# Second attention of a two-network kernel: queries and keys projected with the tokens moving and rotated across partitions, all values projected first

## Chip, cores and metric

One NeuronCore of a Trainium2 chip. The metric is the device time of one execution in microseconds, the median of several runs. The program is one launch: it reads float32 inputs and weights from HBM and writes one output of 256 tokens by 1024.

## The reference

A first block (three mixers, gates, a gated feed-forward layer) and then a second network of two layers, each a mixer and a squared-ReLU MLP, with a norm ahead of and behind each part. Mixer 0 is a retention, mixer 1 the attention that is changed here. With 256 tokens and blocks of 256 it has one block, so its selected part adds only terms that are masked:

```python
q, k, v = jnp.split(h @ w_in, 3, axis=-1)          # 8 heads of 128 each
q = partial_rope(q, pos) * (Dh ** -0.5)
k = partial_rope(k, pos)
...
def partial_rope(x, pos):                          # half = 16, ROPE_DIM = 32
    ...
    x1 = x[..., :half].astype(jnp.float32)
    x2 = x[..., half:ROPE_DIM].astype(jnp.float32)
    rot = jnp.concatenate([x1 * cos - x2 * sin, x2 * cos + x1 * sin], axis=-1)
    return jnp.concatenate([rot.astype(x.dtype), x[..., ROPE_DIM:]], axis=-1)
...
s_own = jnp.einsum('bhnid,bhnjd->bhnij', qb, kb).astype(jnp.float32)
s_own = jnp.where(causal, s_own, NEG)
...                                                # softmax, then p_own @ v
return o.astype(h.dtype) @ w_out
```

So of each head's 128 dimensions the first 16 and the next 16 are rotated against each other by an angle that depends on the token; the other 96 stay.

## The kernel before

**Arithmetic.** Every large product keeps float32 precision by splitting both operands in a high and a low part (float32r): hi·hi + hi·lo + lo·hi. Weights come from HBM in units of 512 KB into six raw buffers. ScalarE writes the high part (whi, a copy), VectorE the low part (wlo = raw - whi), into eight buffers each. `weight(key)` splits three units ahead (AHEAD) of the one it returns; a unit's buffers come free when its last matmul is done (`release`).

**Two ways to project 256 tokens on a chunk of 512 columns.** Two tiles t of 128 are held transposed in hT, high and low part side by side.

- `rows_proj` holds a tile's tokens as stationary operand and moves 512 weight columns: three matmuls of 512 for each of 8 k and each t (`mm3`), 48 for a chunk. The result has tokens in partitions.
- `cols_proj` holds 128 weight columns and moves the tokens: one matmul of 512 columns (both parts of hT) with whi and one of 256 with wlo, for each k, 64 for a chunk. The result has output dimensions in partitions; `two_blocks` does it for two blocks of 128 and adds the two halves (ScalarE copies one, VectorE adds).

**The stage.** Six chunks: values, queries and keys for two groups of four heads, ("m", "v"/"q"/"k", 0 or 1). `keep_split_tile` projects a value tile with rows_proj and writes its split form. `part_rope` (L1406) does a query or key tile: rows_proj into a PSUM tile pj; ScalarE copies the 96 plain dimensions times the token's norm factor; VectorE makes two products with frope (cosine and sine times the factor) into rp and two sums; `heads_T` transposes the four heads on TensorE into a PSUM tile mx, and ScalarE copies them to qT or kT, for queries with the scale 128^-0.5. `probs` then makes logits (two heads at a time, TensorE), adds the causal mask on VectorE, does the softmax, transposes the probabilities and splits them; `mix` multiplies with the values and splits the result into ym. The output projection wo1 (`out_proj`) takes head k of ym with unit k.

The order in the program: v0 and q0 for tile 0, then `flush()` (the MLP's Post chain of tile 1: norm, residual, transposes into hT), then v0 and q0 for tile 1; k0; probs and mix of group 0; q1; k1; probs of group 1; v1; mix of group 1; wo1; Post; the MLP's up chunks 0 and 1 with rows_proj. The factor of a tile (`factors[t]`) is computed by `post.rows(t)`, behind the transposes.

**Who sets the order.** The kernel is recorded twice. The first recording goes to a planner (`Plan`), which knows a cost for each instruction and the dependences, and issues, on each engine, the instruction with the lowest program number among those that are ready (Post chains are advanced by 4000, `urgent`). The order so found is then issued as it stands: each engine runs its own list in order. All instructions are recorded through one line, L213, so the profile's groups are told apart by tiles and shapes. Tiles: pj and mx are PSUM (four buffers each), t is the shared scratch t2 (six buffers), y is hT, ym and split values, p is p4 (qT, kT, probabilities and others), fac the norm factors, sm small statistics, const the constants; "mx<-const,t" is a transpose by the identity.

Of the kernel before, what the change touches and what calls it, by code (L numbers as in the profile page):

```python
# [27 lines left out]
AF = mybir.ActivationFunctionType  # L28
# [273 lines left out]
def host_consts():  # L302
    f = np.float32
    p = np.arange(128)
    s, t = p[:, None], p[None, :]
    same = (s // 64) == (t // 64)
    parts = {}
    parts["ident"] = (s == t).astype(f)
    parts["tri64"] = (same & (s <= t)).astype(f) / f(16)
    parts["late64"] = (same & (s > t)).astype(f) / f(16)  # L310
    parts["ind64"] = (p[:, None] // 64 == np.arange(2)[None, :]).astype(f) / f(16)
    parts["tri"] = (s <= t).astype(f)
    parts["ones"] = np.ones((128, 128), f)
    parts["cmask"] = np.concatenate([np.zeros((128, 128), f), np.where(t > s, f(NEG), f(0))], 1).astype(f)
    pos = np.arange(256, dtype=f)
    inv = np.power(f(500000.0), -np.arange(0, 32, 2, dtype=f) / f(32)).astype(f)
    ang = (pos[:, None] * inv[None, :]).astype(f).astype(np.float64)
    cs = np.stack([np.cos(ang), np.sin(ang)], 1).astype(f)
    parts["rope"] = cs.reshape(2, 128, 2, 16).transpose(1, 0, 2, 3).reshape(128, -1)
    lg = np.log(f(1.0) - np.exp2(-5.0 - np.arange(4, dtype=f)).astype(f)).astype(f)  # L320
    dec = np.zeros((128, 4, 2, 128), f)
    for h in range(4):
        g = np.float64(lg[h])
        dec[:, h, 0] = np.where(t >= s, np.exp(g * np.maximum(t - s, 0)), 0.0)
        dec[:, h, 1] = np.exp(g * (t + 1.0)) * np.exp(g * (127.0 - s))
    parts["dec"] = (dec / 16.0).reshape(128, -1).astype(f)
    freq = (f(1.0) / np.power(f(10000.0), np.linspace(0.0, 1.0, 128, dtype=f))).astype(f)
    ang = (freq[:, None] * pos[None, :]).astype(f).astype(np.float64)
    parts["rot"] = np.concatenate([np.cos(ang), np.sin(ang)], 1).astype(f)
    at, n = {}, 0  # L330
    for k, v in parts.items():
        at[k] = (n, v.shape[1])
        n += v.shape[1]
    return np.ascontiguousarray(np.concatenate(list(parts.values()), 1)), at
# [32 lines left out]
def network(ctx, tc, I, consts, c_at, out, after=None):  # L367
# [30 lines left out]
    def f32(ap):  # L398
        return ap.bitcast(F32)
# [72 lines left out]
    add_chunk("wo0", I["w_out_0_2"], 0, 1024, per=1, nk=16)  # L472
    add_mlp(0)
    base1 = dict(q=0, k=1024, v=2048)
    for kind, j in (("v", 0), ("q", 0), ("k", 0), ("q", 1), ("k", 1), ("v", 1)):
        add_chunk(("m", kind, j), I["w_in_1_2"], base1[kind] + 512 * j, 512)
    add_chunk("wo1", I["w_out_1_2"], 0, 1024, per=1)
    add_mlp(1)

# [15 lines left out]
    def pump(upto):  # L495
        while state["split"] <= min(upto, len(units) - 1) and state["split"] < state["done"] + NSPL:
            i = state["split"]
            load_to(i + NRAW - 1)
            src, kt, n, deint, gain = units[i]
            raw = raws.pop(i)  # L500
            hi = sbt([128, UNIT], "whi", NSPL, F32R)[:, :kt * n]
            lo = sbt([128, UNIT], "wlo", NSPL, F32R)[:, :kt * n]
            if deint:
                src4 = raw.rearrange("p (k m c) -> p k c m", k=kt, c=2)
                hi4, lo4 = [a.rearrange("p (k c m) -> p k c m", k=kt, c=2) for a in (hi, lo)]
                for k in range(kt):
                    S.activation(hi4[:, k], src4[:, k], AF.Copy)
                    V.tensor_tensor(lo4[:, k], src4[:, k], f32(hi4[:, k]), op=OP.subtract)
            elif gain is not None:
                for k in range(kt):  # L510
                    split(hi[:, k * n:(k + 1) * n], lo[:, k * n:(k + 1) * n], raw[:, k * n:(k + 1) * n],
                          g_col[:, gain + k:gain + k + 1])
            else:
                split(hi, lo, raw)
            spl[i] = (cols(hi, n), cols(lo, n))
            state["split"] += 1
        load_to(state["split"] + NRAW - 1)
# [225 lines left out]
    def probs(qT, kT, kind, hp, bias=None):  # L743
# [4 lines left out]
        for t in range(2):  # L748
# [4 lines left out]
            if kind == "cross":  # L753
                L = sp
            else:
                L = cols(t2(), 256)
                if kind == "fox":
                    V.tensor_tensor(L[:, :, :W], sp[:, :, :W], bias[t][:, 2 * hp:2 * hp + 2, :W], op=OP.subtract)
                else:
                    V.tensor_tensor(L[:, :, :W], sp[:, :, :W],  # L760
                                    cmask[:, None, 256 - W:].to_broadcast([128, 2, W]), op=OP.add)
            m, nm, l, r = small(2), small(2), small(2), small(2)
            V.tensor_reduce(m, L[:, :, :W], axis=AX, op=OP.max)
            V.tensor_scalar(nm, m, -1.0, None, op0=OP.mult)
# [636 lines left out]


    plan.table(nc, "natural_log_exp_and_others")
    rope = const("rope").rearrange("p (t c n) -> p t c n", t=2, c=2)
    frope = sbt([128, 2, 2, 16], "frope", 1)
    def part_rope(key, t, dst, scale):  # L1406
        p = pj()
        rows_proj(key, hT, t, p, 0, 512)
        src = cols(p, 128)
        q = t2()  # L1410
        qh = cols(q, 128)
        S.activation(qh[:, :, 32:], src[:, :, 32:], AF.Copy, scale=factors[t][0])
        a, b = [sbt([128, 4, 2, 16], "rp", 4) for _ in range(2)]
        for o, c in ((a, 0), (b, 1)):
            V.tensor_tensor(o, src[:, :, :32].rearrange("p h (c n) -> p h c n", c=2),
                            frope[:, t, c][:, None, None, :].to_broadcast([128, 4, 2, 16]), op=OP.mult)
        V.tensor_tensor(qh[:, :, :16], a[:, :, 0], b[:, :, 1], op=OP.subtract)
        V.tensor_tensor(qh[:, :, 16:32], a[:, :, 1], b[:, :, 0], op=OP.add)
        heads_T(q, dst, t, scale)

    QS = float(128 ** -0.5)
    ym = []
    v, qT, kT = new_v(), cols(p4(), 256), cols(p4(), 256)
    for t in range(2):
        if t:
            flush()
        V.tensor_scalar(frope[:, t], rope[:, t], factors[t][0], None, op0=OP.mult)
        keep_split_tile(v, ("m", "v", 0), hT, t, factors[t][0])
        part_rope(("m", "q", 0), t, qT, QS)
    release_chunk(("m", "v", 0), 4)  # L1430
    release_chunk(("m", "q", 0), 4)
    for t in range(2):
        part_rope(("m", "k", 0), t, kT, None)
    release_chunk(("m", "k", 0), 4)
    ym.append(new_y())
    for hp in range(2):
        mix(probs(qT, kT, "moba", hp), v, ym[0], "moba", hp)
    qT, kT = cols(p4(), 256), cols(p4(), 256)
    for kind, dst, sc in (("q", qT, QS), ("k", kT, None)):
        for t in range(2):  # L1440
            part_rope(("m", kind, 1), t, dst, sc)
        release_chunk(("m", kind, 1), 4)
    pTs = [probs(qT, kT, "moba", hp) for hp in range(2)]
    v = keep_split(("m", "v", 1), hT, [f for f, _ in factors])
    ym.append(new_y())
    for hp in range(2):
        mix(pTs[hp], v, ym[1], "moba", hp)
# [72 lines left out]
```

## Time and profile before

| | us |
|---|---|
| median of 3 runs | 1137.17 (1136.91 to 1137.51) |
| the profiled execution | 1138.05 |
| its span in the trace | 1136.3 |
| TensorE busy | 1125.8 |
| VectorE busy | 822.5 |
| ScalarE busy | 649.9 |
| GpSimd busy | 6.0 |

Busy times are unions of the listed durations. Matmuls overlap their neighbours, so a matmul's cost is read as the distance from its start to the next one's. The stage lies between about 838 and 947 us of the span. Times in the rows count from the start of the span.

### The profile page before, as it was taken

The numbers are of one execution on the slowest core, as the hardware profiler recorded it, in microseconds if no ns is written. First come the engines' busy times: TensorE is split into PE (matmuls) and PEld (weight loads), VectorE is DVE, ScalarE is ACT, GpSimd is POOL, SyncE is SP. The second block draws the span as 40 slices with busy tenths as digits, with TensorE's granted clock in tenths as the row PEclk, the third lists the DMA queues.
The fourth block names the chain that finished last, engine by engine and source line by source line (L and its number), as shares of the span: only waits on it lengthen the run. The fifth ranks groups of instructions, "written<-read, shape, count | busy, mean of one in ns | idle before, by whom it ended". The sixth has DMA issues, their size and how long they took to land.

```text
span 1136.3 us, 15881 instructions
## 1 busy us (share of the span) xinstructions
PE 1125.8 (99%) x5852; PEld 953.1 (84%) x5852; DVE 822.5 (72%) x1487; ACT 649.9 (57%) x1068; POOL 6.0 (1%) x18
## 2 busy tenths in 40 slices
PE   9999999999999999999999999999999999999997
PEld 7989888888988888888888888888888888888885
DVE  6998797897656566787858497656588889755564
ACT  6867657675645554646556474545466667545451
POOL 1000000000000000000000000000000000000000
PEclk9999999999999999999999999999999999999999
DMA  8654546665666664665464448564637354665631
GB/s 306 212 161 125 164 136 184 217 227 172 204 187 191 190 192 127 198 211 186 150 209 159 134 161 281 167 206 152 217 118 254 115 175 136 223 192 185 215 113 38
DMA packets 100756, 204.23 MB, mean 180 GB/s; under 512 B 6533, under 2 KB 30150, under 8 KB 100678
## 3 DMA queue, kind: packets, MB, share of 16 engines
q1 hardware_dynamic: 99814, 202.17, 55.1%
q10 hardware_dynamic: 864, 1.05, 0.3%
q8 instruction: 46, 0.75, 0.3%
q14 instruction: 32, 0.26, 0.1%
HBM read 202.14 MB, written 1.05 MB: 179 GB/s over the span
## 4 chain that ended last, share of the span: by engine, by line
PE 94%; DVE 2%; DMA 2%; ACT 1%; issue 0%; SPq 0%; DVEq 0%; ACTq 0%
PE pj L213 62%; PE mx L213 32%; DVE wlo L213 1%; DMA p<-in_ln_mlp_post_dram 1%; DMA raw<-in_w_in_dram 1%; DMA raw<-in_w_down_dram 1%; DVE p L213 0%; DVE t L213 0%; ACT whi L213 0%; DVE sm L213 0%; SPq L213 0%; ACT t L213 0%; DMA x<-in_x_dram 0%; DVE y L213 0%; DVE x L213 0%
## 5 line engine op out<-in xcount | busy, mean ns | idle before, releaser
L213 PE MATMUL pj<-whi,y 128*128 128x512 f32 (+2 forms) x1744 | 543.6, 388 | 0.0
L213 DVE TENSOR_TENSOR wlo<-raw,whi 128x1024 fp32r<-128x1024 f32 (+1 forms) x326 | 378.0, 1170 | 125.6 <-ACT whi L213 121.4
L213 ACT ACTIVATE whi<-raw 128x1024 fp32r<-128x1024 f32 (+1 forms) x326 | 327.1, 1019 | 122.3 <-PE pj L213 91.2
L213 PEld LDWEIGHTS pj<-whi,y 128*128 128x128 f32 x1744 | 321.7, 188 | 65.9 <-issue 0.3
L213 PE MATMUL pj<-wlo,y 128*128 128x512 f32 (+2 forms) x872 | 337.3, 387 | 0.6 <-DVE wlo L213 0.6
L213 PE MATMUL mx<-y,whi 128*128 128x512 f32 x672 | 236.8, 396 | 0.0
L213 PEld LDWEIGHTS pj<-wlo,y 128*128 128x128 f32 x872 | 164.0, 188 | 33.2 <-DVE wlo L213 1.4
L213 PE MATMUL mx<-y,wlo 128*128 128x256 f32 x672 | 188.5, 281 | 0.0
L213 PEld LDWEIGHTS mx<-y,whi 128*128 128x128 f32 x672 | 126.1, 188 | 29.9
L213 PE MATMUL pj<-y,whi 128*128 128x512 f32 x416 | 146.3, 395 | 0.0
L213 PEld LDWEIGHTS mx<-y,wlo 128*128 128x128 f32 x672 | 126.5, 188 | 0.8
L213 PE MATMUL pj<-y,wlo 128*128 128x256 f32 x416 | 116.5, 280 | 0.0
L213 PEld LDWEIGHTS pj<-y,whi 128*128 128x128 f32 x416 | 78.1, 188 | 18.1
L213 DVE SCALAR_TENSOR_TENSOR wlo<-raw,gcol,whi 128x512 fp32r<-128x512 f32 (+2 forms) x120 | 85.0, 747 | 5.5 <-ACT whi L213 3.8
L213 ACT ACTIVATE t<-mx 128x256 f32<-128x256 f32 (+1 forms) x106 | 41.5, 396 | 81.4 <-PE mx L213 81.2
L213 ACT ACTIVATE whi<-raw,gcol 128x512 fp32r<-128x512 f32 (+2 forms) x120 | 79.8, 719 | 14.4 <-PE pj L213 10.7
L213 PEld LDWEIGHTS pj<-y,wlo 128*128 128x128 f32 x416 | 78.2, 188 | 0.1
L213 DVE TENSOR_TENSOR t<-mx,t 128x256 f32<-128x256 f32 x88 | 37.1, 422 | 51.0 <-ACT t L213 51.0
L213 PE MATMUL mx<-whi,y 128*128 128x256 f32 (+1 forms) x256 | 64.5, 340 | 0.0
L213 ACT ACTIVATE t<-pj 128x256 f32<-128x256 f32 (+1 forms) x74 | 29.7, 401 | 55.6 <-PE pj L213 42.1
L213 PEld LDWEIGHTS mx<-whi,y 128*128 128x128 f32 x256 | 43.7, 189 | 5.0
L213 ACT ACTIVATE y<-t 128x512 fp32r<-128x512 f32 x33 | 20.9, 633 | 45.0 <-DVE t L213 45.0
(143 smaller groups left out, 861.9 us busy)
## 6 DMA issues: line engine op xcount, KB each, us to landing
raw<-in_w_in_dram SPq DMA_DIRECT2D x115, 512.0 KB, 4.5
raw<-in_w_up_dram SPq DMA_DIRECT2D x64, 512.0 KB, 4.9
raw<-in_w_down_dram SPq DMA_DIRECT2D x64, 512.0 KB, 4.7
raw<-in_w_out_dram SPq DMA_DIRECT2D x32, 512.0 KB, 4.1
raw<-in_w_ffn_gate_dram SPq DMA_DIRECT2D x22, 512.0 KB, 4.2
raw<-in_w_ffn_up_dram SPq DMA_DIRECT2D x22, 512.0 KB, 4.3
raw<-in_w_ffn_down_dram SPq DMA_DIRECT2D x22, 512.0 KB, 3.7
raw<-in_w_branch_dram SPq DMA_DIRECT2D x12, 512.0 KB, 4.5
```

Of the source, the lines that this page charges most:

```text
L213: self.ops[i]()
```

## The change

Constants: a table ropeT, 128 partitions by 2 by 256 tokens: row 0 is the cosine in partitions 0 to 15 and 64 to 79 and 1 elsewhere, row 1 is minus the sine in 0 to 15 and the sine in 64 to 79, 0 elsewhere. It is loaded by DMA into the buffer of the retention's rot table.

Weights: the order of the six chunks becomes v0, v1, q0, k0, q1, k1. The units of queries and keys are split with their columns moved: of each head's eight groups of 16 columns the even ones come first, so that the two rotated groups land at columns 0 and 64. Each unit takes two copies on ScalarE and two subtractions on VectorE where it took one of each.

part_rope: for each chunk twice (two heads at a time), two_blocks; a scratch tile u is zeroed by GpSimd, ScalarE copies the rotated groups to each other's partitions in u; VectorE multiplies the projection by row 0 of ropeT, u by row 1, and adds. No factor per token, no transposes. The factors of both tiles are broadcast, transposed on TensorE into a PSUM tile fp and multiplied into ropeT, once. The scale of the queries moves into the logits, where the mask is added.

Values: both groups are projected at the beginning, for tile 0 and, behind flush(), for tile 1, into two tiles vm.

```diff
-    for kind, j in (("v", 0), ("q", 0), ("k", 0), ("q", 1), ("k", 1), ("v", 1)):
-        add_chunk(("m", kind, j), I["w_in_1_2"], base1[kind] + 512 * j, 512)
+    for kind, j in (("v", 0), ("v", 1), ("q", 0), ("k", 0), ("q", 1), ("k", 1)):
+        add_chunk(("m", kind, j), I["w_in_1_2"], base1[kind] + 512 * j, 512, deint="even" if kind in "qk" else False)
...
+            elif even:
+                for b in range(2):
+                    src4, hi4, lo4 = [a.rearrange("p (h a n) -> p h a n", a=8, n=16) for a in (raw, hi, lo)]
+                    src4, hi4, lo4 = src4[:, :, b::2], hi4[:, :, 4 * b:4 * b + 4], lo4[:, :, 4 * b:4 * b + 4]
+                    S.activation(hi4, src4, AF.Copy)
+                    V.tensor_tensor(lo4, src4, f32(hi4), op=OP.subtract)
...
-                    V.tensor_tensor(L[:, :, :W], sp[:, :, :W],
-                                    cmask[:, None, 256 - W:].to_broadcast([128, 2, W]), op=OP.add)
+                    V.scalar_tensor_tensor(L[:, :, :W], sp[:, :, :W], float(128 ** -0.5),
+                                           cmask[:, None, 256 - W:].to_broadcast([128, 2, W]),
+                                           op0=OP.mult, op1=OP.add)
...
+    ropeT = cols(load_const("ropeT", sbt([128, 512], "rot", 1)), 256)
+
+    def part_rope(key, dst):
+        for i in range(2):
+            s = two_blocks(key, hT, pj, 256 * i)
+            u = cols(t2(), 256)
+            G.memset(u, 0.0)
+            S.activation(u[:16], s[64:80], AF.Copy)
+            S.activation(u[64:80], s[:16], AF.Copy)
+            o = dst[:, 2 * i:2 * i + 2]
+            V.tensor_tensor(o, s, ropeT[:, 0:1].to_broadcast([128, 2, 256]), op=OP.mult)
+            V.tensor_tensor(u[:80], u[:80], ropeT[:80, 1:2].to_broadcast([80, 2, 256]), op=OP.mult)
+            V.tensor_tensor(o[:80], o[:80], u[:80], op=OP.add)
+        release_chunk(key, 4)
...
+    vm, fp = [new_v(), new_v()], mx()
     for t in range(2):
         if t:
             flush()
-        V.tensor_scalar(frope[:, t], rope[:, t], factors[t][0], None, op0=OP.mult)
-        keep_split_tile(v, ("m", "v", 0), hT, t, factors[t][0])
-        part_rope(("m", "q", 0), t, qT, QS)
...
+        for j in range(2):
+            keep_split_tile(vm[j], ("m", "v", j), hT, t, factors[t][0])
+        fc = t2()[:, :128]
+        V.tensor_copy(fc, factors[t][0].to_broadcast([128, 128]))
+        T.transpose(fp[:, t * 128:(t + 1) * 128], fc, ident)
+    V.tensor_tensor(ropeT, ropeT, fp[:, None, :256].to_broadcast([128, 2, 256]), op=OP.mult)
...
+    part_rope(("m", "q", 0), qT)
+    part_rope(("m", "k", 0), kT)
+    v = vm[0]
...
-    for kind, dst, sc in (("q", qT, QS), ("k", kT, None)):
-        for t in range(2):
-            part_rope(("m", kind, 1), t, dst, sc)
-        release_chunk(("m", kind, 1), 4)
+    part_rope(("m", "q", 1), qT)
+    part_rope(("m", "k", 1), kT)
     pTs = [probs(qT, kT, "moba", hp) for hp in range(2)]
-    v = keep_split(("m", "v", 1), hT, [f for f, _ in factors])
+    v = vm[1]
```

## Rows read from the trace of the kernel before

**Rows 1.** The page, busy time of each engine over the span

```profile
span 1136.3 us, 15881 instructions
...
PE 1125.8 (99%) x5852; PEld 953.1 (84%) x5852; DVE 822.5 (72%) x1487; ACT 649.9 (57%) x1068; POOL 6.0 (1%) x18
```

**Rows 2.** The page, the chain that ended last, by engine

```profile
PE 94%; DVE 2%; DMA 2%; ACT 1%; issue 0%; SPq 0%; DVEq 0%; ACTq 0%
```

**Rows 3.** Stretches: width, busy us (count) of PE, PEld, DVE, ACT, POOL; clock; DMA

```profile
838.00:866.00 28.00, 28.00 (x129) 22.87 (x128) 26.53 (x51) 19.99 (x32) 0.63 (x2) 1.00 0.67 213
866.00:956.00 90.00, 90.00 (x463) 75.54 (x462) 75.40 (x206) 58.39 (x127) 0.62 (x2) 1.00 0.51 168
912.00:931.40 19.40, 19.40 (x108) 16.63 (x107) 18.80 (x57) 15.93 (x38) 0.00 (x0) 1.00 0.43 143
975.00:1060.00 85.00, 84.79 (x424) 71.39 (x425) 51.81 (x64) 38.85 (x51) 0.00 (x0) 1.00 0.59 193
```

**Rows 4.** Timeline of PE, old and new form: start, length, operation, count

```profile
700.08 0.39 PE L213 MATMUL pj<-wlo,y 128*128 128x512 f32 x1
...
713.92 0.39 PE L213 MATMUL pj<-wlo,y 128*128 128x512 f32 x1
...
715.07 0.39 PE L213 MATMUL mx<-y,whi 128*128 128x512 f32 x1
...
722.10 0.39 PE L213 MATMUL mx<-y,whi 128*128 128x512 f32 x1
```

**Rows 5.** Timeline of PE around one group of heads_T

```profile
858.02 0.60 PE L213 MATMUL mx<-const,t 128*128 128x128 f32 x4
858.38 0.71 PE L213 MATMUL pj<-whi,y 128*128 128x512 f32 x2
858.93 0.39 PE L213 MATMUL pj<-wlo,y 128*128 128x512 f32 x1
```

**Rows 6.** Timeline of DVE, old part_rope and splits

```profile
854.03 0.49 DVE L213 TENSOR_TENSOR rp<-pj,frope 128x128 f32<-128x128 f32 x2
854.43 1.22 DVE L213 TENSOR_TENSOR x<-p,x 128x1024 f32<-128x1024 f32 x1
855.56 0.23 DVE L213 TENSOR_TENSOR t<-rp 128x64 f32<-128x64 f32 x1
855.70 1.22 DVE L213 TENSOR_TENSOR wlo<-raw,whi 128x1024 fp32r<-128x1024 f32 x1
856.83 0.22 DVE L213 TENSOR_TENSOR t<-rp 128x64 f32<-128x64 f32 x1
```

**Rows 7.** Timeline of DVE in the retention stage, whose rotation lies across partitions

```profile
483.66 0.68 DVE L213 TENSOR_TENSOR wlo<-raw,whi 128x512 fp32r<-128x512 f32 x1
484.26 0.74 DVE L213 SCALAR_TENSOR_TENSOR y<-pj,fac,y 128x512 fp32r<-128x512 f32 x1
...
489.29 1.29 DVE L213 TENSOR_TENSOR t<-t,rot 128x512 f32<-128x512 f32 x2
...
495.16 0.42 DVE L213 TENSOR_TENSOR t<-pj,t 128x256 f32<-128x256 f32 x1
495.50 1.22 DVE L213 TENSOR_TENSOR wlo<-raw,whi 128x1024 fp32r<-128x1024 f32 x1
```

**Rows 8.** Timelines of POOL and of DVE around one memset

```profile
887.85 0.31 POOL L213 MEMSET t<- 128x256 f32 x1 [28.80 <-DVE sm L213]
...
886.41 0.72 DVE L213 TENSOR_SCALAR t<-t,sm 128x256 f32<-128x256 f32 x2
...
887.86 0.76 DVE L213 TENSOR_SCALAR t<-t,sm 128x256 f32<-128x256 f32 x2
```

**Rows 9.** PE's groups from 909.5 to 932.1: count, then busy us, mean ns

```profile
L213 PE MATMUL pj<-whi,y 128*128 128x512 f32 x45 | 15.5, 403 | 0.0
L213 PE MATMUL pj<-wlo,y 128*128 128x512 f32 x23 | 9.2, 401 | 0.0
```

More of the change, by code (lines that the diff above doesn't have):

```diff
@@ L326, in host_consts @@
     parts["dec"] = (dec / 16.0).reshape(128, -1).astype(f)
+    ang = (pos[:, None] * inv[None, :]).astype(f).astype(np.float64).T
+    rr = np.ones((128, 2, 256), f)
+    rr[:, 1] = 0
+    for a, sign in ((0, -1), (64, 1)):
+        rr[a:a + 16, 0], rr[a:a + 16, 1] = np.cos(ang), sign * np.sin(ang)
+    parts["ropeT"] = rr.reshape(128, -1)
     freq = (f(1.0) / np.power(f(10000.0), np.linspace(0.0, 1.0, 128, dtype=f))).astype(f)
@@ L499, in pump @@
             src, kt, n, deint, gain = units[i]
+            deint, even = deint is True, deint == "even"
             raw = raws.pop(i)
@@ L1403, in network @@
     plan.table(nc, "natural_log_exp_and_others")
[L1404 to L1419, printed above, removed]
+    ropeT = cols(load_const("ropeT", sbt([128, 512], "rot", 1)), 256)
[11 more added lines that the diff above has]
+        release_chunk(key, 4)
     QS = float(128 ** -0.5)
     ym = []
-    v, qT, kT = new_v(), cols(p4(), 256), cols(p4(), 256)
+    vm, fp = [new_v(), new_v()], mx()
     for t in range(2):
@@ L1426, in network @@
             flush()
-        V.tensor_scalar(frope[:, t], rope[:, t], factors[t][0], None, op0=OP.mult)
-        keep_split_tile(v, ("m", "v", 0), hT, t, factors[t][0])
-        part_rope(("m", "q", 0), t, qT, QS)
-    release_chunk(("m", "v", 0), 4)
-    release_chunk(("m", "q", 0), 4)
-    for t in range(2):
-        part_rope(("m", "k", 0), t, kT, None)
-    release_chunk(("m", "k", 0), 4)
+        for j in range(2):
[4 more added lines that the diff above has]
+    V.tensor_tensor(ropeT, ropeT, fp[:, None, :256].to_broadcast([128, 2, 256]), op=OP.mult)
+    for j in range(2):
+        release_chunk(("m", "v", j), 4)
+    qT, kT = cols(p4(), 256), cols(p4(), 256)
+    part_rope(("m", "q", 0), qT)
+    part_rope(("m", "k", 0), kT)
+    v = vm[0]
     ym.append(new_y())
@@ L1438, in network @@
     qT, kT = cols(p4(), 256), cols(p4(), 256)
-    for kind, dst, sc in (("q", qT, QS), ("k", kT, None)):
-        for t in range(2):
-            part_rope(("m", kind, 1), t, dst, sc)
-        release_chunk(("m", kind, 1), 4)
+    part_rope(("m", "q", 1), qT)
+    part_rope(("m", "k", 1), kT)
     pTs = [probs(qT, kT, "moba", hp) for hp in range(2)]
-    v = keep_split(("m", "v", 1), hT, [f for f, _ in factors])
+    v = vm[1]
     ym.append(new_y())
```

## The prediction

> **What bounds the kernel now.** I read the page first: its busy table gives TensorE 1125.8 of 1136.3 us and VectorE 822.5 [rows 1], and the chain that ended last is 94% TensorE [rows 2]. So the whole kernel is set by the matmul stream; every other engine counts only where it makes that stream wait. Then I went to the stage that is changed, by stretches [rows 3]: from 866 to 956, which holds the query and key chunks, both softmax rounds, the output projection and the first up chunks behind it, TensorE is full for 90.00 of 90 us, and VectorE is busy for 75.40. VectorE's rest is uneven: in the softmax round at the end of the stage, 912 to 931.4, it is busy 18.80 of 19.40, in the stretch ahead of the stage 26.53 of 28.00, but from 975 on only 51.81 of 85. The reader should see two engines near their limits here and one with room behind it. The last views are timelines, for what single instructions cost in a row; there I take the distance from one start to the next, since the listed durations overlap.
>
> The profiled execution took 1138.05 us, 0.88 over the median of the runs (1137.17). The sum is made on the former and 0.88 is taken off. What a measurement here can tell from no change is 0.2%, or 2.27 us.
>
> **TensorE's side.** Old projection: 16 triples of 512 columns for a chunk. Twenty triples run from 700.08 to 713.92, so 0.692 each and 11.07 a chunk. New projection (two_blocks): 32 pairs of 512 and 256 columns. Twenty pairs run from 715.07 to 722.10, so 0.352 each and 11.25 a chunk [rows 4]. The columns are the same in number; four chunks cost 4 x 0.18 = 0.7 more. The value chunks are only moved: no change.
>
> heads_T goes, with eight groups of four transposes. One group: it starts at 858.02, the next matmul at 858.38, and the two matmuls behind it take 0.55 to the next start, against 2/3 of 0.692 = 0.46. So 0.36 + 0.09 = 0.45, times 8 = 3.6 removed [rows 5]. The factors' two transposes into fp come back at about 0.09 + 0.09 each, 0.4. TensorE therefore saves 3.6 - 0.7 - 0.4 = 2.5 us, if it never waits.
>
> **VectorE's side.** It loses, for each of eight old tiles, two products and two sums: two products start at 854.03 and the next instruction at 854.43, so 0.40; one sum holds 855.56 to 855.70, so 0.14, and the other the same [rows 6]. That is 0.68 a tile, 5.4 in all. The two frope instructions are smaller still: 0.3.
>
> It gains, for each of eight halves of part_rope: two adds out of PSUM, 0.34 each (495.16 to 495.50), and three SBUF operations over 512 elements, 0.60 each (483.66 to 484.26; the rotary products of retention, 1.29 for two, have the same size) [rows 7]. 2 x 0.34 + 3 x 0.60 = 2.48, times 8 = 19.8. That two of these cover only 80 partitions I cost as 128: the trace has no row that tells. Splitting a query or key unit in two costs 2 x 0.60 instead of one operation of 1.13 (855.70 to 856.83) [rows 6, 7]: 0.07 x 16 = 1.1. Its runs of 16 elements are not in the trace in this size; the retention's split that reads every second element is the 0.60 row itself, so I take no penalty; were it as long as the 1024 one, 16 x 1.06 = 17 more, which I hold unlikely. ropeT times the factors is 0.6, the two copies of a factor 0.2 each by the 0.14 and 0.34 rows. The logits become a scalar_tensor_tensor; the nearest such row lasts 0.74 where a plain one lasts 0.68 [rows 7], so 0 to 8 x 0.06 = 0.5; I take 0.
>
> VectorE's sum: 19.8 - 5.4 - 0.3 + 1.1 + 0.6 + 0.4 = 16.2 us more, all of it between about 866 and the end of the stage.
>
> **What this does to the stream.** VectorE's idle time from 866 to 956 is 90 - 75.40 = 14.6. All of its work there must be done by about 956: splits of weights for wo1 and the first two up chunks, the softmax, the Post chain. What is behind, from 975 on, has 39% idle and can take no part of it, since TensorE needs these results first. Busy would be 75.4 + 16.2 = 91.6. An in-order engine that waits for others can't be filled wholly: in the softmax round it is idle for 0.60 of 19.40 or 3.1%, ahead of the stage for 1.47 of 28 or 5.3% [rows 3]. I take 3.1%, the row of the same work: 91.6 / 0.969 = 94.5 us for what now takes 90, while TensorE would need 87.5. VectorE becomes the bound of this stretch, and TensorE waits about 7 us in it. The splits run ahead of their matmuls (up to eight buffers); I allow 1 us of that lead to be eaten. Net 94.5 - 90 - 1 = +3.5: 1138.05 + 3.5 = 1141.55 in profile, less 0.88 = **1140.7**.
>
> Bounds: with no idle at all 91.6 - 90 - 1 = +0.6; with 5.3% 96.7 - 90 - 1 = +5.7; the 0.5 of the logits goes on top. The likeliest case's own range is 1137.8 to 1143.4.
>
> **What I cost at nothing.** ScalarE: two instructions more in each of 8 halves and 16 more for the splits, 32 at its mean of 58.39 / 127 = 0.46, 15 us; it is idle for 31.6 of the 90 [rows 3]. If that cover fails, it is the same wait again, one link earlier. GpSimd: eight memsets of 512 elements, about twice the 0.31 of the 256 one [rows 8], on an idle engine; they start before the copies need them. The ropeT load is 0.26 MB beside 168 GB/s x 90 us = 15 MB [rows 3], into a buffer free since the retention stage; it has to land before the second tile's factor, which lands late anyway. Values at the beginning: the value chunk of head group 1 takes the place of query chunk 0 as cover while the second tile's Post chain runs, so that cover stays; queries wait for both tiles' factors only behind their matmuls.
>
> The memsets are also where a rule speaks against the change. In the trace one memset (887.85, 0.31) falls on two VectorE tensor_scalars that then last 0.76 together, against 0.72 for the same pair without it (886.41): 0.04 us [rows 8]. The Trainium skill ("SBUF — State Buffer", "SBUF: two separate sides") says that VectorE and GpSimd share a port pair as an exclusive lock, and that the loser "fully blocks". By that rule eight memsets of some 0.6 could hold VectorE for up to 5 us, and the sum would be about 1145.5; by the row it is 8 x 0.08 = 0.6 at most, and I add nothing.
>
> **Rivals.** *TensorE stays the bound.* If VectorE's work packs better than I think (splits drop back to just in time, deferred work flows past 956), the 2.5 us saved is all that is left: 1138.05 - 2.5 - 0.88 = 1134.7. For it: TensorE has no gap from 866 to 931 although VectorE is at 97% at the end [rows 3]. Against it: 91.6 into 87.5 doesn't go, so at least 4 us would have to slip behind 956. It decides as soon as 5 us of splits can be later than now without being missed. This is also what a rule would give: the Trainium skill ("Perfetto Trace Analysis", "Identifying Performance Opportunities") has a kernel improve by relieving its most-contended engine, which by occupancy is TensorE, at 99% of the page's span; the trace agrees for the kernel as a whole and not for this stretch.
>
> *The softmax is left without cover.* From 909.5 (the last transposes of the keys) to 932.1 (the last split of the mix, after which wo1's second half can run) TensorE has 68 projection matmuls of 0.231, 15.7 us [rows 9]; the other 6.9 of the 22.6 are the attention's own. Up to 48 of the 68 are the second value chunk, which is moved away. What can fill in is wo1 for the first four heads, 48 matmuls or 11.1 us, so 6.9 + 11.1 = 18.0 of 22.6: a wait of 4.6. Against it: the first two heads of the group finish earlier and free another 24 matmuls, 5.5 us. On top of VectorE's excess it gives 1140.7 + 4.6 = 1145.3; alone, less the 2.5 saved, 1139.3.
>
> *Half hidden.* 4 to 6 of the 7 us of waiting vanish into the lead of the splits: 1134.7 plus 1 to 3, 1136 to 1138.
>
> **Chances.** VectorE bound 0.50 (of this 0.10 within 2.27 us of before); TensorE bound 0.20 (1134.7 lies just past the limit of 1134.9, so half of it counts as faster, half as same); half hidden 0.13, same; uncovered softmax 0.17, of it 0.03 same. Slower 0.40 + 0.14 = 0.54, same 0.10 + 0.10 + 0.13 + 0.03 = 0.36, faster 0.10. The range reaches from the TensorE case to the uncovered one: 1134.3 to 1145.5.
>
> **What would show it.** Right: the 512-and-256 pairs at 0.35 and no groups of four transposes between the projections; VectorE busy for some 91 of the stretch that starts with the first query chunk, idle under 5%; TensorE with gaps of about 7 us in sum, released by VectorE (wlo, p, y or the logits), most between the last key chunk and the first up chunk; GpSimd's memsets without lengthened VectorE operations beside them. Wrong: TensorE as dense as now and the stage 2.5 us shorter (then the 16 us went into idle time and lead); VectorE's operations over 80 partitions or in 16-element runs with other durations; a gap at the stage's beginning, before the first query chunk, which I don't expect at all; waits for the ropeT load.

## The result, and the profile after

The changed kernel takes 1147.09 us (median of four runs, 1145.64 to 1149.30) beside 1137.20 for the kernel before on the same chip: ratio 1.0090, 95% interval 1.0078 to 1.0102. It is 9.9 us slower, where 3.5 were forecast, and outside the range. The profiled execution took 1146.93 us, 8.88 more than that of before, and 8.9 of it is in the span. The page, busy times and the chain:

```profile
span 1145.2 us, 16031 instructions
...
PE 1127.8 (98%) x5886; PEld 955.2 (83%) x5886; DVE 837.5 (73%) x1512; ACT 658.0 (57%) x1100; POOL 10.2 (1%) x26
...
PE 92%; DVE 4%; DMA 2%; ACT 1%; issue 0%; SPq 0%; DVEq 0%; ACTq 0%
```

Against [rows 1, 2] VectorE has 15.0 us more work (16.2 were forecast), and the chain that ended last has handed 2% of the span from TensorE to VectorE. The stretches show where; the columns are those of [rows 3], and the last four rows divide the end of the stage:

```profile
838.00:866.00 28.00, 28.00 (x135) 23.02 (x134) 26.81 (x57) 19.80 (x38) 1.94 (x4) 1.00 0.64 209
866.00:956.00 90.00, 81.73 (x447) 68.54 (x446) 83.01 (x215) 63.45 (x146) 3.36 (x8) 0.98 0.52 169
...
912.00:932.00 20.00, 19.03 (x98) 15.44 (x97) 19.14 (x63) 17.59 (x45) 0.31 (x1) 1.00 0.53 179
932.00:948.00 16.00, 14.14 (x64) 10.63 (x63) 14.60 (x24) 5.83 (x10) 0.00 (x0) 1.00 0.65 213
948.00:954.00 6.00, 0.83 (x5) 0.55 (x4) 4.30 (x11) 4.70 (x11) 0.00 (x0) 0.81 0.75 273
954.00:960.00 6.00, 5.73 (x20) 4.48 (x19) 5.55 (x14) 3.32 (x6) 0.00 (x0) 0.62 0.00 0
```

TensorE was busy for 90.00 of the 90 us from 866 to 956; now it is busy for 81.73, so 8.3 us of waiting. Of these 2.8 lie in the softmax round (0.97 before 932, 1.86 up to 948) and over 5 in one piece behind 948. From 954 to 960 the granted clock is 0.62 in the mean, so part of these 6 us ran at the lower of its two levels (1.2 and 2.4 GHz). VectorE, which was to be the bound, is busy for 83.01 of the 90 us and idle for 7. TensorE's timeline at the end of the stage (start, length, operation, count, idle time ahead of it and what ended it):

```profile
938.90 0.39 PE L213 MATMUL mx<-p,y 128*128 128x256 f32 x1 [0.47 <-ACT p L213]
939.45 0.97 PE L213 MATMUL mx<-p,y 128*128 128x256 f32 x6 [0.17 <-DVE p L213]
940.92 0.85 PE L213 MATMUL mx<-p,y 128*128 128x256 f32 x5 [0.49 <-DVE p L213]
942.46 0.50 PE L213 MATMUL pj<-whi,y 128*128 128x512 f32 x1 [0.69 <-ACT y L213]
...
947.89 0.40 PE L213 MATMUL pj<-whi,y 128*128 128x512 f32 x1
953.46 1.12 PE L213 MATMUL mx<-const,t 128*128 128x128 f32 x4 [5.17 <-DVE t L213]
954.84 1.12 PE L213 MATMUL mx<-const,t 128*128 128x128 f32 x4 [0.27 <-DVE sm L213]
...
957.46 0.63 PE L213 MATMUL mx<-wlo,y 128*128 128x512 f32 x1
957.89 0.63 PE L213 MATMUL mx<-whi,y 128*128 128x512 f32 x1
```

The matmuls "mx<-p,y" of mix wait for one probability tile after another. Behind 947.89 the output projection wo1 is used up, for both tiles, and nothing is left to do until the first tile's Post chain has its transposes ready at 953.46. Behind this gap a matmul of 512 columns takes 0.43 (957.46 to 957.89) instead of 0.231, a third of the triple of 0.692 in [rows 4]. Before, TensorE had no gap here. The place of the last splits says why; first before, then after, VectorE's splits that end the two mixes ("y<-mx,y"), which wo1's second half needs:

```profile
927.85 0.68 DVE L213 TENSOR_TENSOR y<-mx,y 128x512 fp32r<-128x512 f32 x1
931.39 0.68 DVE L213 TENSOR_TENSOR y<-mx,y 128x512 fp32r<-128x512 f32 x1
```

```profile
932.59 0.69 DVE L213 TENSOR_TENSOR y<-mx,y 128x512 fp32r<-128x512 f32 x1
...
943.05 0.68 DVE L213 TENSOR_TENSOR y<-mx,y 128x512 fp32r<-128x512 f32 x1
```

The last split ends at 943.73 instead of 932.07. That it is later is no sign by itself, since the 11.1 us of the second value chunk now run ahead of it; what counts is what is left behind it. Before, wo1 went on to about 947, 15 us behind the last split. After, with no value chunk behind the last keys, 72 of wo1's 96 matmuls ran under the softmax (from 913.31 to 938), and the rest is done at 948, some 4 us behind the last split; there is nothing left to stand under the Post chain.

### The profile page after: what moved, and what is told of

It is laid out like the page before. It is cut to its first block, busy times and chain, and to the rows that moved or that the text cites. A ratio compares the mean times of both kernels' runs of the same rounds, so it can differ in the third digit from the quotient of the medians.

```text
span 1145.2 us, 16031 instructions
## 1 busy us (share of the span) xinstructions
PE 1127.8 (98%) x5886; PEld 955.2 (83%) x5886; DVE 837.5 (73%) x1512; ACT 658.0 (57%) x1100; POOL 10.2 (1%) x26
## 3 DMA queue, kind: packets, MB, share of 16 engines
q10 hardware_dynamic: 864, 1.05, 0.3%
HBM read 202.40 MB, written 1.05 MB: 178 GB/s over the span
## 4 chain that ended last, share of the span: by engine, by line
PE 92%; DVE 4%; DMA 2%; ACT 1%; issue 0%; SPq 0%; DVEq 0%; ACTq 0%
PE pj L213 59%; PE mx L213 33%; DVE p L213 1%; DVE wlo L213 1%; DVE t L213 1%; DMA const<-consts_dram 1%; DVE sm L213 1%; DMA p<-in_ln_mlp_post_dram 1%; DMA raw<-in_w_in_dram 1%; ACT t L213 0%; SPq L213 0%; ACT whi L213 0%; DMA x<-in_x_dram 0%; DVE y L213 0%; ACT y L213 0%
## 5 line engine op out<-in xcount | busy, mean ns | idle before, releaser
L213 PE MATMUL pj<-whi,y 128*128 128x512 f32 (+3 forms) x1616 | 502.1, 387 | 0.8 <-ACT y L213 0.7
L213 PEld LDWEIGHTS pj<-whi,y 128*128 128x128 f32 x1616 | 298.2, 188 | 63.0 <-ACT y L213 1.3
L213 PE MATMUL pj<-wlo,y 128*128 128x512 f32 (+2 forms) x808 | 311.4, 386 | 0.4 <-DVE wlo L213 0.3
L213 PE MATMUL pj<-y,whi 128*128 128x512 f32 x544 | 191.5, 395 | 0.0
L213 PEld LDWEIGHTS pj<-wlo,y 128*128 128x128 f32 x808 | 151.9, 188 | 30.9 <-DVE wlo L213 1.0
L213 PE MATMUL pj<-y,wlo 128*128 128x256 f32 x544 | 152.4, 281 | 0.0
L213 PEld LDWEIGHTS pj<-y,whi 128*128 128x128 f32 x544 | 102.0, 188 | 23.2
L213 PEld LDWEIGHTS pj<-y,wlo 128*128 128x128 f32 x544 | 102.2, 188 | 0.2
L213 ACT ACTIVATE whi<-raw,gcol 128x512 fp32r<-128x512 f32 (+2 forms) x120 | 79.8, 716 | 14.6 <-PE pj L213 10.8
L213 ACT ACTIVATE t<-pj 128x256 f32<-128x256 f32 (+1 forms) x90 | 35.6, 397 | 60.0 <-PE pj L213 49.4
L213 PE MATMUL mx<-const,t 128*128 128x128 f32 (+1 forms) x265 | 42.1, 278 | 5.8 <-DVE t L213 5.5
```

What stands on the lines that cost most here:

```text
L213: self.ops[i]()
```

## The experiments

Two theories. **Cover**: what counts is the matmuls that are free to run behind the last key chunk: the value chunk that was moved away (48 matmuls of 0.231, 11.1 us) and wo1. They carry first the last softmax, then the Post chain; with the value chunk gone the chains lie open. **Work**, the prediction's: VectorE has 15 us more to do in a stretch where it has 14.6 idle, and sets the pace. Rivals on single points are the place of a small instruction (e4), the clock (e5) and the stage's beginning (e18). Differences below are medians against the kernel before on the same chip, intervals those of the ratio.

### The two halves apart

**e1**: the kernel before, old rotation, with all values first.

```diff
-    for kind, j in (("v", 0), ("q", 0), ("k", 0), ("q", 1), ("k", 1), ("v", 1)):
+    for kind, j in (("v", 0), ("v", 1), ("q", 0), ("k", 0), ("q", 1), ("k", 1)):
...
+        for j in range(2):
+            keep_split_tile(vm[j], ("m", "v", j), hT, t, factors[t][0])
...
-    v = keep_split(("m", "v", 1), hT, [f for f, _ in factors])
+    v = vm[1]
```

> The kernel before with one part of the change alone: all values projected at the beginning; queries and keys keep the old rotation and its transposes. Work theory (the 16 us that VectorE gains set the time): nothing was added to VectorE, so within 2 us of before, 1136 to 1139. Cover theory (the 11.1 us of value matmuls that ran under the softmax are missing there, so wo1 is used up under it and nothing is left for the Post chain): most of the loss appears without the new rotation, 1142 to 1148, with a gap of several us on TensorE between the last wo1 matmul and the first transposes for the MLP.

Measured: 1142.93, +5.8 (1.0034 to 1.0064). The move alone costs more than half of the whole, though it adds no instruction. Its stretch, and 6 us of it:

```profile
866.00:956.00 90.00, 87.31 (x431) 72.51 (x431) 69.69 (x197) 56.81 (x123) 0.94 (x3) 0.96 0.49 158
...
936.00:942.00 6.00, 5.53 (x20) 4.70 (x20) 5.42 (x8) 1.97 (x5) 0.00 (x0) 0.50 0.29 88
```

TensorE waits 2.7 us here, 1.05 at most in one piece (ahead of a matmul of mix at 933.27), while VectorE has 20 us to spare: no lack of VectorE. The gap of several us behind wo1 that I expected isn't there. Much of the rest of the loss is the clock, which is at its lower level from 936 to 942, behind the first waits. That comes and goes between executions: this one (1144.79) and another (1143.66) have 0.996 over the span, the other two (1142.20 and 1141.19) 0.999 and 0.998. The two pairs are 2.5 us apart in the mean, and the faster one loses 4.6.

**e2**: the new rotation for k0, q1 and k1, second value chunk last as before; the first query chunk keeps the old projection, and since its columns are in the old order, the first group's logits are not the attention's. **e9** is the same with the column order mended.

```diff
-    part_rope(("m", "q", 0), qT)
+    part_rope_rows(("m", "q", 0), t, qT, None)
...
-    v = vm[1]
+    v = keep_split(("m", "v", 1), hT, [f for f, _ in factors])
```

> The new rotation for three of the four chunks (k0, q1, k1), with the order of before: v0 and q0 first (q0 in the old form, by tiles), v1 under the softmax of group 1. VectorE gets 3/4 of the added work, 12 us. Work theory: 75.4 + 12 = 87.4 busy of 90, at 3% idle 90.2, less 1 of lead: between 1136 and 1140, and with the excess measured so far (10 instead of 3.5) rather 1140 to 1144. Cover theory: no gap behind wo1; 1135 to 1138, the transposes saved and some waits in the softmax.

> Three of the four query and key chunks in the new rotation, the first query chunk token-rows with the old rotation but in the new column order, the second value chunk last as before. Same work as e2_values_last, with the attention's own logits. Cost of the two halves simply adds: as e2, 1140.5 to 1142. If the position of the values does not matter and VectorE's work sets the time: 3/4 of +10, 1144 to 1145.

Measured: e2 1141.14, +4.0 (1.0022 to 1.0051); e9 1140.26, +3.4 (1.0019 to 1.0045). For e2 the cover theory as I put it missed (1135 to 1138, no gap): TensorE waits 4.4 us from 942 to 954 although the value chunk is back, and the time lies in the work theory's later range. The two halves, 5.8 and 3.4 to 4.0, come near the 9.9 of both, which looked like two independent costs. They are not, as e13 and e17 show below.

**e3**: the kernel after without the memset, the two copies, the sine product and the sum (9.6 us of VectorE's work), so the sine part of the rotation is left out.

```diff
-            V.tensor_tensor(u[:80], u[:80], ropeT[:80, 1:2].to_broadcast([80, 2, 256]), op=OP.mult)
-            V.tensor_tensor(o[:80], o[:80], u[:80], op=OP.add)
```

> The changed kernel without the cross terms of the rotation (no memset, no copies between partitions, no product with the sine, no sum: only the product with the cosine stays). It takes 8 x 1.2 = 9.6 us from VectorE and 8 x 1.27 = 10 from ScalarE. Work theory: 9 of the 10 us lost come back, 1137 to 1139. Cover theory: the chain behind the last key chunk gets some 3 us shorter, the gap behind wo1 stays: 1142 to 1145.

Measured: 1144.15, +7.0 (1.0045 to 1.0075). Three fifths of the added VectorE work gone give 2.9 of 9.9 back.

### How much of the rotation, and which

With the second value chunk last, as before: **e10** k0 and q1 in the new form, **e14** these and q0, **e16** k1 alone, **e11** all four (the kernel after with the value chunk put back). For a chunk in the old form:

```diff
-    part_rope(("m", "k", 1), kT)
+    for t in range(2):
+        part_rope_rows(("m", "k", 1), t, kT, None)
+    release_chunk(("m", "k", 1), 4)
```

> As e9, but the second key chunk too is projected as token rows with the old rotation, so that only k0 and q1 have the new one (about 8 us more of VectorE instead of 12), and the last key's rotation before the final softmax is the old, short one. VectorE's work alone: two thirds of e9's excess, 1139.5 to 1140. The latency behind the last key chunk: excess nearly gone, 1137 to 1138.5. No change against e9 would mean that neither counts.

> e11 (all new rotation, second value chunk last as before) with only the second key chunk in the old form: token rows, old rotation, transposes. VectorE has about 12 us more than before instead of 16. Amount of work: three quarters of e11's 3.6, 1139.5 to 1140. Place of the last key: 1135 to 1137, as e10 or, with two more groups of transposes gone, a little less.

> Only the second key chunk in the new rotation, the three other chunks in the old form, second value chunk last as before: VectorE has only about 4 us more than before. Amount of work: a quarter of the rotation's cost, 1137 to 1138. Place of the last key: nearly all of it, 1139.5 to 1141.

> The kernel after with only the second value chunk moved back behind the last keys: all four chunks in the new rotation. If the move of the values costs what e1 shows (5.8) and the rotation the rest: 1141 to 1142.5. Against it, the start of the stage now has one value half-chunk (5.5 us) instead of two under the second tile's Post chain, so a new wait of 1 to 4 us ahead of 866: 1142.5 to 1146. If only VectorE's work counts: 1147, no change.

| new rotation for | median us | against before | 95% of the ratio | VectorE's busy time added, us | last split of mix starts |
|---|---|---|---|---|---|
| none (before) | 1137.2 | | | | 931.39 |
| e10: k0, q1 | 1135.67 | -1.2 | 0.9980 to 0.9998 | 7.0 | 930.45 |
| e14: q0, k0, q1 | 1135.12 | -1.8 | 0.9972 to 0.9991 | 10.1 | 932.54 |
| e16: k1 | 1137.74 | +0.8 | 0.9995 to 1.0014 | 4.0 | 935.33 |
| e9: k0, q1, k1 | 1140.26 | +3.4 | 1.0019 to 1.0045 | 11.2 | 936.34 |
| e11: all | 1140.43 | +3.6 | 1.0019 to 1.0039 | 13.9 | 934.52 |

e11 first: with the value chunk put back, 6.3 us of the slowdown are gone (9.9 less 3.6, each against its own before), and the kernel stands at 1140.43, where the prediction had 1140.7 for the whole change. The wait ahead of 866 that I had set against it is not there: TensorE is busy for 27.97 of 28.00 us from 838 to 866.

Then the last key. Three chunks without it are faster than before, and by what the prediction's sum for TensorE gives (2.5 for four, so 1.9 for three). e10 lies below both ranges that I had given it. With k1 on top -1.2 turns into +3.4 and -1.8 into +3.6. e14 and e9 have the same number of chunks and nearly the same work; only which chunk differs. So it is not the amount alone: k1's softmax is the last of the stage, and what comes late there comes late for wo1. The last column goes with it: where the last split starts at up to 932.5 TensorE has no wait behind wo1, at 934.5 and later it has. Alone, though, k1 costs at most 1.6 and perhaps nothing (e16), where I expected nearly all; what it needs beside it is not shown. The stretches of e14, e9 and e11 (the trace of e9 is its slowest execution, 1142.61, with a clock of 0.96, that of e11 its fastest, 1139.11):

```profile
866.00:956.00 90.00, 90.00 (x479) 76.41 (x478) 86.30 (x220) 62.95 (x141) 1.99 (x5) 1.00 0.56 181
```

```profile
866.00:956.00 90.00, 85.83 (x457) 72.96 (x456) 85.30 (x215) 61.79 (x139) 3.18 (x7) 0.96 0.53 170
```

```profile
866.00:956.00 90.00, 86.94 (x464) 72.63 (x463) 86.41 (x218) 64.05 (x142) 2.98 (x7) 1.00 0.52 166
```

In all three VectorE is busy for 95 or 96% of the stretch; only e14 has TensorE without a gap.

### VectorE's work by itself

**e12** and **e13** add three products of 128x512 behind each of the eight old rotations of the kernel before, whose results nobody reads; in e13 they read the rotation's result. **e17** is e13's addition on e1.

```diff
         V.tensor_tensor(qh[:, :, 16:32], a[:, :, 1], b[:, :, 0], op=OP.add)
+        for _ in range(3):
+            V.tensor_tensor(burn, q, q, op=OP.mult)
```

> The kernel before, unchanged in order and in TensorE's work, with three VectorE products of 128x512 whose result nobody reads behind each of the eight rotations (24 x 0.6 = 14.4 us, about what the change added). VectorE's work by itself, as the prediction had it: waits of 3 to 5 us, 1140 to 1142. If it is the length of the chain behind the last key and the lost cover and not the amount: within 1 us of before, 1137 to 1138.

> The kernel before with three VectorE products of 128x512 behind each of the eight rotations, which now read the rotation's result, so that they stand in the changed stage (24 x 0.6 = 14.4 us there); nobody reads what they write. TensorE's work and the order of the chunks are those of before. VectorE's amount of work sets the time, as the prediction had it: 3 to 5 us more, 1140 to 1142. Only the length of what stands behind the last key counts: the three products behind the last rotation delay its softmax by up to 1.8, 1137 to 1139.

> e1 (before with all values first, old rotation) with e13's three VectorE products of 128x512 behind each of the eight rotations, read by nobody. If the second value chunk behind the last keys is the reserve out of which VectorE's work was paid: e1's 1142.9 plus 2 to 5, 1145 to 1148. If VectorE's amount of work costs nothing here either, as in e13: 1142 to 1143.5, and the rotation's cost with the values first is its own chain's alone.

e12 missed: its products depend on nothing, so the planner put them at the kernel's start (the trace has them from 2.5 to 118.1 us), and its 1138.26 (+1.4, 1.0004 to 1.0023) tells nothing of this stage. e13 has them from 857.7 to 911.2, at 0.68 each. Measured: 1136.69, -0.25 (0.9988 to 1.0007), no change. e17: 1149.39, +12.5 (1.0099 to 1.0129), 6.6 more than e1 (each against its own before). Their stretches, e13 first:

```profile
866.00:956.00 90.00, 90.00 (x462) 75.48 (x461) 86.26 (x228) 58.83 (x127) 0.62 (x2) 1.00 0.51 163
```

```profile
866.00:956.00 90.00, 82.97 (x419) 67.75 (x418) 82.17 (x220) 55.15 (x122) 0.94 (x3) 1.00 0.52 165
```

The same dead work costs nothing where the value chunk stands behind the last keys and 6.6 us where it doesn't. Up to 86 of 90 us VectorE's amount has no price of its own here. It makes the last split start 2.1 us later (933.50 in e13) and is paid out of the cover; without that it is paid in time, although VectorE then has 7.8 us idle in the stretch. More than 86.4 of 90 was in no run: the 91.6 of the prediction was not tried (e13 adds 12.1 us over the whole kernel, the rotation 15).

**e15**: the kernel after with only k1 in the old form, values first.

> The kernel after with only the second key chunk back in the old form; all values stay at the beginning. If the last key's rotation costs the same here as with the values last (e9 against e10: 4.6): 1142 to 1143.5, what the values alone cost in e1. If the values' move is the whole of it and the last key hides: 1146 to 1147. If the two multiply: under 1141.

Measured: 1145.53, +8.6 (1.0059 to 1.0089), outside all three expectations: taking the last key back gives 1.3 to 1.6, where the same step gives 5.4 with the values last. Values first costs 10.4 between e14 and e15, 12.7 between e13 and e17, 6.3 between e11 and the kernel after, and 5.8 with the old rotation. So neither part has one price; the move costs most where VectorE's added work had been free before.

### Is it the place, or the beginning?

**e18**: the kernel before with only the second value chunk moved, between the first keys and the second queries, not to the stage's beginning.

```diff
     release_chunk(("m", "k", 0), 4)
+    v1 = keep_split(("m", "v", 1), hT, [f for f, _ in factors])
...
-    v = keep_split(("m", "v", 1), hT, [f for f, _ in factors])
+    v = v1
```

> The kernel before, old rotation, with only the second value chunk moved: projected between the first keys and the second queries, not at the stage's beginning. If what e1 lost is the cover under the last softmax round: about as e1, 1141 to 1144. If it is the beginning (the order of loads and splits there, four more units ahead of the queries): within 1 us of before, 1136.5 to 1138.

Measured: 1141.38, +4.4 (1.0023 to 1.0051), with nothing changed at the beginning. That is three quarters of e1's cost, and as much as e1's two executions at the higher clock lose (4.6); e18's five are all at 0.998 or 0.999. So the place that is left counts, and no loss remains that the beginning would have to explain. The waits in its timeline are those of e1, at mix and behind it:

```profile
932.80 0.38 PE L213 MATMUL mx<-p,y 128*128 128x256 f32 x1 [1.04 <-ACT p L213]
934.69 0.38 PE L213 MATMUL mx<-p,y 128*128 128x256 f32 x1 [0.26 <-ACT p L213]
...
951.09 0.50 PE L213 MATMUL mx<-whi,y 128*128 128x512 f32 x1 [0.90 <-ACT y L213]
```

The Trainium skill ("Perfetto Trace Analysis", "Optimization Strategy") says that where the most-contended engine changes over time, interleaving the regimes can help. That speaks against this change, which takes the projection out of the softmax round, and e1 and e18 agree with it, by 5.8 and 4.4 us.

### Mending the open chain

**e6**: the kernel after with wo1's second half for the second tile in another order, so that heads whose splits come last are used first and the others are kept. **e4**: the kernel after with the product of the last norm's gain, which stands in ScalarE's list in the gap at 949.65, moved into a later step. **e5**: the kernel after with 26 matmuls of low priority whose result nobody reads, to fill the gap.

```diff
-        for k in range(2, KT):
+        for n, k in enumerate((2, 3, 4, 5, 6, 7) if not t else (6, 7, 2, 3, 4, 5)):
```

> The changed kernel with one order turned: tile 1's second half of wo1 begins with heads 6 and 7, so that none of it can run under the softmax; its 36 matmuls (8.3 us) all stay behind tile 0's as cover for the Post chain. Cover theory: the gap of 5.3 us behind wo1 and the slow clock after it (2.4) go; the waits under the softmax grow by the 24 matmuls that filled there, 5.5 us: 1144 to 1146, and the place of the wait moves ahead of the last mix. Work theory: VectorE sets the time wherever TensorE waits, 1147.

> The changed kernel with the last gain row (ln_mlp_post_1) loaded and scaled behind the first up chunks instead of ahead of them. In the changed kernel ScalarE waits 1.09 us for this row and scales it for 1.06 between the two squares of the first Post chain, while TensorE waits 5.3 us for that chain. Both theories: the chain starts its second square 2 us earlier, the gap is 3.3 us, 1144.5 to 1145.5. Rival: the second square isn't what the chain waits for, no change, 1147.

```diff
+    for _ in range(26):
+        T.matmul(idle, ym[1][0][:, 3, :128], hT.both(0), start=True, stop=True)
```

> The changed kernel with 26 more matmuls of 512 columns (6.0 us, results unused) that become ready when the second group's last heads are done and that only fill what TensorE would idle behind wo1. The wait for the Post chain stays as long as it is, but TensorE is busy in it. Clock theory: the granted clock, 0.62 from 954 to 960 in the changed kernel, stays at 1.00 there and the 427 ns matmuls behind the gap return to 231: 2.4 us less, 1144.5 to 1145. Rival: those matmuls are slow since they wait for VectorE's splits; no change, 1147.

e6: 1146.06, +8.6; its interval, 1.0058 to 1.0092, takes in the 1.0090 of the changed kernel. The gap behind wo1 is closed, and the waits are under the softmax instead; its stretches from 912 to 956:

```profile
912.00:932.00 20.00, 16.55 (x81) 13.03 (x81) 19.14 (x63) 16.81 (x41) 0.31 (x1) 0.98 0.56 184
932.00:948.00 16.00, 13.33 (x61) 10.11 (x61) 12.06 (x23) 3.85 (x12) 0.00 (x0) 0.92 0.53 165
948.00:956.00 8.00, 8.00 (x41) 6.55 (x40) 7.12 (x14) 7.93 (x13) 0.00 (x0) 1.00 0.24 67
```

Waiting is 6.1 us from 912 to 956 as against 8.3: cover can be moved, hardly made. e4: 1147.05, +9.9, no change, where 1144.5 to 1145.5 was expected: a weight copy of 1.04 took the free place, and the first transposes start at 953.39 instead of 953.46. e5: 1146.57, +9.1 (1.0066 to 1.0096). 19 of its matmuls lie in the gap, and the granted clock stays at 1.00:

```profile
948.00:954.00 6.00, 5.04 (x24) 3.88 (x23) 4.07 (x10) 4.60 (x12) 0.00 (x0) 1.00 0.78 283
954.00:960.00 6.00, 6.00 (x32) 4.98 (x30) 5.83 (x14) 3.49 (x6) 0.00 (x0) 1.00 0.00 0
```

The time is 0.5 us less, where 2.4 were expected, and its interval takes in the changed kernel's 1.0090 too, so even that is not clear of noise. The second tile's transposes come 1.5 us earlier (963.84 for 965.36), but their third group starts at 968.19 instead of 968.31, so something else sets that, and the slow clock costs little here. What it is I did not follow.

### The sine part on GpSimd

**e7** puts the sine product and the sum of the kernel after on GpSimd; **e8** does it in e9.

```diff
-            V.tensor_tensor(u[:80], u[:80], ropeT[:80, 1:2].to_broadcast([80, 2, 256]), op=OP.mult)
-            V.tensor_tensor(o[:80], o[:80], u[:80], op=OP.add)
+            G.tensor_tensor(u[:80], u[:80], ropeT[:80, 1:2].to_broadcast([80, 2, 256]), op=OP.mult)
+            G.tensor_tensor(o[:80], o[:80], u[:80], op=OP.add)
```

> The changed kernel with the product with the sine and the sum done by GpSimd instead of VectorE (16 operations of 80 x 512); nothing is left out. VectorE has 9.6 us less, ScalarE the same work as in the changed kernel. If they cost GpSimd about 1 us each, as the experiment without the cross terms, which came to 1144.2: 1143 to 1145.5. Rival: the two engines disturb each other or GpSimd is so slow (over 2 us each) that the last key heads come later: 1147 or more.

> The second experiment (new rotation for k0, q1 and k1, values of group 1 last) with query chunk 0 in the same column order as its keys and the sine product and the sum on GpSimd: VectorE has 12 - 7 = 5 us more than before instead of 12. The cover is there as before; what eats it is how much later the mix ends. If the 4 us of the second experiment go with VectorE's added work, 5/12 of 4 plus the saving that was in it: 1137 to 1139. Rival: the chain behind the last keys is longer by the form itself (two copies across partitions, GpSimd's two steps), 1140 to 1142.

Measured: e7 1153.90, +16.4 (1.0122 to 1.0161); e8 1146.63, +9.1 (1.0063 to 1.0093), against +3.4 for e9. Both are worse than with VectorE; e8 lies outside both of its ranges. e7's timelines of GpSimd and VectorE:

```profile
888.88 1.29 POOL L213 TENSOR_TENSOR t<-t,rot 80x512 f32<-80x512 f32 x1 [3.53 <-ACT t L213]
...
908.63 1.52 POOL L213 TENSOR_TENSOR t<-t,rot 80x512 f32<-80x512 f32 x1 [3.30 <-ACT t L213]
910.23 1.27 POOL L213 TENSOR_TENSOR p<-p,t 80x512 f32<-80x512 f32 x1
```

```profile
889.22 1.05 DVE L213 TENSOR_SCALAR sm<-sm 128x2 f32<-128x2 f32 x2
...
908.95 3.41 DVE L213 TENSOR_SCALAR t<-t,sm 128x256 f32<-128x256 f32 x2
```

One operation takes 1.3 to 1.75 on GpSimd where VectorE needs 0.68, and some of VectorE's own stand still meanwhile: the pair that takes 0.72 in [rows 8] takes 3.41 and ends at 912.36, after both GpSimd operations are over (911.50). Not all do: a reduction at 890.18, beside GpSimd's sum from 890.25 to 891.54, takes its usual 0.67. The Trainium skill ("SBUF — State Buffer", "SBUF: two separate sides") has the port pair of the two engines as an exclusive lock; for VectorE operations with two SBUF inputs it binds only against GpSimd operations that read SBUF. The prediction's 5 us for the memsets left this condition out. The traces agree: a VectorE sum of two small SBUF tiles at 903.50 takes 0.92 instead of 0.15 and ends with GpSimd's (903.12 to 904.41), while a memset, which reads nothing, leaves a product of 80x512 beside it (from 900.00, the memset from 900.09 to 900.62, in the kernel after) at 0.68.

## Why the prediction was wrong, by its steps

**TensorE's side.** Right. The pairs of 512 and 256 columns stand at 0.35, and e14, three of four chunks with no new wait, is 1.8 faster where the sum gives 1.9.

**VectorE's side.** Right as a sum: 15.0 for 16.2. The kernel after, groups from 860 to 925 (count, busy time, mean ns):

```profile
L213 DVE TENSOR_TENSOR wlo<-raw,whi 128x512 fp32r<-128x512 f32 x24 | 15.6, 682 | 0.0
...
L213 DVE TENSOR_TENSOR t<-t,rot 80x512 f32<-80x512 f32 x8 | 5.5, 686 | 2.6 <-ACT t L213 2.6
L213 DVE TENSOR_TENSOR p<-t,rot 128x512 f32<-128x512 f32 x8 | 5.5, 683 | 0.1
L213 DVE TENSOR_TENSOR p<-p,t 80x512 f32<-80x512 f32 x8 | 5.4, 678 | 0.0
```

80 partitions last as long as 128, and runs of 16 elements as long as contiguous ones (682 against the 0.68 of [rows 7]), both as costed.

**What this does to the stream.** The number held for the rotation by itself: +3.5 forecast, +3.6 in e11. As far as the runs show, that is luck: this step failed too. I divided work by capacity and had TensorE wait 7 us; in e11's trace it waits 3.1. And e13 and e14 have VectorE busy for 86.3 of 90 with no wait, e9 for 85.30 with 4.2 us of waiting, the kernel after for 83.01 with 8.3. What makes TensorE wait is how late the last mix is split against how many free matmuls are left, and no busy share tells that. Where the work stood mattered more than how much it was: VectorE's part of all but the last key chunk was free (e14).

**"Values at the beginning ... so that cover stays": the step that failed.** It was costed at nothing and costs 6.3 (e11 against the kernel after; 5.8 in e1 without the rotation), which is the miss of 6.4. I looked only at the cover in the place where the chunk goes, the second tile's Post chain, and that was right: no gap stands there. At the place that it leaves I counted one wait, as the rival of the uncovered softmax, and priced that at 4.6. The softmax does wait, 2.8 us by busy time; what I left out comes behind it. Under the softmax three quarters of wo1 are spent, which had stood under the next Post chain, and that chain lies open for 5.2 us: wo1 goes on for 4 us behind the last split instead of 15. I took the fillers as free, where the one that closes most of a wait is borrowed from the next chain.

**The rivals.** The uncovered softmax was the right family and, on top of the sum, near in size (1145.3 for 1147.09), at a chance of 0.17; but its 4.6 was to be a wait in the softmax, where 2.8 were measured, and most of the waiting came one chain further than I followed it. "TensorE stays the bound", 1134.7, is about what the rotation does without its last key and without the move: 1135.12. Half hidden didn't occur.

**Costed at nothing.** ScalarE's busy time rose by 8.1, not 15, with no wait of TensorE for it above 0.69; no wait for the ropeT load is in the trace; the memsets cost next to nothing (the longest effect seen is a tensor_scalar pair at 890.41, beside one of them, of 0.86 where [rows 8] has 0.72).

What stays open: why k1 costs 0.8 alone and 5.4 on top of the three others, and how much of e11's 3.6 is VectorE's amount. The list of instructions that the planner makes differs in each of these kernels, and in e9 weight splits of 1.22 us each stand between the last softmax operations; I didn't test another order.

## What to carry to other kernels

Before a block of matmuls is moved, write down for the place that it leaves which chain ran under it, and then which chain ran under the work that will fill in for it; the bill comes at the end of that line, where nothing is left to borrow. A busy share near one is not yet a bound, nor idle time a proof of room: test an amount by adding dead work where it would stand, with a dependence that keeps it there. If half of a change costs the cover, keep the other half: the new rotation for all but the last keys, with the values left where they were (e14, 0.9982, interval 0.9972 to 0.9991), beats both kernels.

## What the runs showed of the hardware

After 5.2 us with no matmul the granted clock was 0.62 for the next 6 us (948 to 954: 0.81), and a 512-column matmul took 0.43 instead of 0.231; matmuls in the gap whose result nobody reads kept it at 1.00. Shorter waits brought the clock down in one execution and not in another: behind waits of 1.05 and 0.26 us e1 shows 0.50 from 936 to 942, and behind waits of 1.04 and 0.26 e18 shows 1.00. A GpSimd product of 80x512 in float32 takes 1.3 to 1.75 us, about twice VectorE's 0.68, and two GpSimd operations in a row stretched a VectorE pair from 0.72 to 3.41, while a reduction beside one of them kept its 0.67.
